# One base address modulo 4096 for all matmul operand tiles of a two-layer decoder trunk

## The chip, the cores and the metric

The kernel runs on one core of one Trainium2 chip. The metric is the device time of one execution in microseconds (us); the time of a kernel is the median of several runs. The profile is of one execution on the same chip.

## What is computed

Two layers over 512 tokens of width 1024, in float32. Each layer is a normed mixer with a residual and a normed feed-forward part with a residual:

```
for l in range(2):
    h = rmsnorm(x, g_pre_mix[l])
    z = h @ w_in[l]                      # 1024 -> 2312: mLSTM q,k,v,o,gates; attention q,k,v
    m_out = mlstm_chunkwise(...)         # 4 heads, 4 chunks of 128 tokens
    a_out = sliding_window_attention(...)# 8 query heads, 2 key heads, window 128, sinks, rotary
    x = x + rmsnorm(concat(m_out, a_out) @ w_out[l], g_post_mix[l])
    h = rmsnorm(x, g_pre_ffn[l])
    u = causal_dwconv(h @ w_up[l], ffn_conv_w[l])       # 1024 -> 5632, width 3
    gate, val = u[:, :2816], u[:, 2816:]
    x = x + rmsnorm((silu(gate) * val) @ w_down[l], g_post_ffn[l])
```

## The kernel before, in words

Every large product is done in split precision. An operand is stored as two tiles, a rounded high part and the rest, and one product takes three matmuls: high by high, high by low, low by high (`mm3`, line 111). So one 128x128 block of weights against 512 columns costs three matmuls of 512 columns each. In the names of an instruction, `acc<-g,w` is a matmul into an accumulator `acc`, with `g` the operand that is streamed through the array (512 columns) and `w` the one that is loaded into it (128 columns).

Weights come by DMA from SP into a `raw` tile; ACT writes the high part and DVE the low part (`wsplit`, lines 98 to 106). The parts land in tiles of four pools, each 128 rows high:

- `hp` (8 tiles `h`) and `wp` (6 tiles `w`), 1024 words per row, and `rp` (3 tiles `raw`), 1024 words;
- `gp` (21 tiles `g`), the main pool, `SLOT` = 1032 words per row (line 29). It holds the transposed activations of the feed-forward part, the outputs of the mixer, part of the gated activations, some weights, and two tiles per layer for the values of the mLSTM (lines 248 and 249), each with two blocks of 4x129 = 516 words. 2x516 = 1032 is why a slot is that wide.

The pools are laid one behind the other in a row of SBUF, so the width of a slot sets the byte address of every tile. In the built program the 21 `g` tiles begin at 40544 + 4128·i, the `h` tiles at 127232 + 4096·i, the `w` tiles at 160000 + 4096·i, and `raw` behind them. So every `h`, `w` and `raw` tile begins at 256 modulo 4096, while the `g` tiles begin at 3680, 3712, 3744, ..., each 32 bytes further modulo 4096 than the one before. A matmul of 512 columns reads both its operands at a multiple of 512 bytes from a tile's start.

The stages of a layer, and which pools their two operands have: the projections by channel (`zchans`, streamed `h`, loaded `w`: `acc<-h,w`) and by token (`ztok`, `acc<-w,h`, 384 columns; `head`, 392 columns); attention and mLSTM in small matmuls between these; the output projection (`outproj`: `acc<-h,g`, `acc<-g,g`, `acc<-w,g`); the up projection (lines 762 to 785: `acc<-g,w`, streamed activations in `g`, 44 blocks of 24 matmuls, the first three blocks in halves of 256 columns); the down projection (lines 801 to 824: streamed weights in `w`, or in `g` for the last five steps of the second half, and the gated activations loaded, `h` for the first four of eleven steps and `g` for the rest; `acc` in the first half, `aux` in the second).

The order on each engine is that of the code; a tile that is wanted waits until the earlier user of its slot is done. POOL issues some small DMAs (`g<-wk`, `g<-g`: halves of the queries and keys moved to other partitions, lines 384 and 400). The descriptors of POOL's DMAs stand in a scratch at the bottom of SBUF, 16 KB in each partition.

Of the kernel before, what the change touches and what calls it, by code (L numbers as in the profile page):

```python
# [8 lines left out]
F32 = mybir.dt.float32  # L9
# [9 lines left out]
NT = 4  # L19
DFF = 2816  # L20
NK2 = 11
NTAIL = 5
# products of the mixer's projections between the steps of the gates, before attention, and between those of the mLSTM
GF = (8, 3, 4, 6)
START = 34
MF = (3, 2, 3, 3, 2)
EPS = 1e-6
NEG = -1e30
SLOT = 1032
WRK = 520  # L30

# columns of the constants
C_ID = 0
C_TRI = 128
C_SEL = 256
# [3 lines left out]
C_MCAU = 528  # L39
C_N = 656  # L40

# columns of the parameters of a layer
P_QK = 0
P_FF = 20
P_SINK = 152
# [5 lines left out]
def tile_hymba_trunk(ctx: ExitStack, tc, x, wch, wta, wtb, wout, wup, wdn, par, gv, mhg, cst, rope, out):  # L51
    nc = tc.nc
    NOSYNC = mybir.DependencyInfo(mybir.DependencyClass.NoSync, mybir.DependencyReason.DATA)

    def after(ins, prev):
        if prev is not None:
            tc.add_manual_dep(ins.ins, prev.ins.name, NOSYNC, reason="slots")
        return ins

    keep = ctx.enter_context(tc.tile_pool(name="keep", bufs=1))  # L60
    gp = ctx.enter_context(tc.tile_pool(name="gp", bufs=21))
    hp = ctx.enter_context(tc.tile_pool(name="hp", bufs=8))
    wp = ctx.enter_context(tc.tile_pool(name="wp", bufs=6))
# [8 lines left out]
    def nm(s):  # L72
        cnt[0] += 1
        return f"{s}_{cnt[0]}"

    def slot(dt=F32, pool=None):
        pool = pool or gp
        if pool is gp:
            t = gp.tile([128, SLOT], dt, tag="g", name=nm("g"))
        elif pool is hp:  # L80
            t = hp.tile([128, 1024], dt, tag="h", name=nm("h"))
        else:
            t = wp.tile([128, 1024], dt, tag="w", name=nm("w"))
        return t

    def work(dt=F32):
        return wk.tile([128, WRK], dt, tag="wk", name=nm("wk"))

# [6 lines left out]
    def small(n, tag):  # L95
        return sp.tile([128, n], F32, tag=tag, name=nm(tag), bufs=1 if n >= 16 else 4)
# [17 lines left out]
    def split_evac(ps, hi, lo):  # L114
        i = nc.scalar.activation(hi, ps, AF.Copy)  # L115
        return i, nc.vector.tensor_tensor(lo, ps, hi.bitcast(F32), ALU.subtract)

    # constants
    cs = keep.tile([128, C_K], F32, name="cs")
    ident = cs[:, C_ID:C_ID + 128]  # L120
    tri = cs[:, C_TRI:C_TRI + 128]
# [29 lines left out]
    def gload(l, i, eng=None, gate=None):  # L151
        g = gbp.tile([128, D], F32, tag="gb", name=nm("gb"))
        after((eng or nc.gpsimd).dma_start(g, gv[l, i:i + 1, :].to_broadcast([128, D])), gate)
        return g
# [57 lines left out]
    def layer_consts(l, gate):  # L212
        pt = keep.tile([128, P_N], F32, tag=f"par{l}", name=f"par{l}")
        after(nc.gpsimd.dma_start(pt, par[l]), gate)
        gh = keep.tile([128, 512], F32, tag="gh", name=f"gh{l}")
        after(nc.gpsimd.dma_start(gh, mhg[l:l + 1, :].to_broadcast([128, 512])), gate)
        ns = keep.tile([128, 8], F32, tag=f"ns{l}", name=f"ns{l}")
        nc.gpsimd.tensor_scalar(ns, pt[:, P_SINK:P_SINK + 8], -1.0, None, ALU.mult)
        return pt, gh, ns
# [13 lines left out]
    def head_weights(l, units, gate, gate2=None):  # L233
        return [wsplit(wta[l, u], 784, wp if u < 2 else gp, gate, gate2)[0] for u in units]
# [4 lines left out]
    def start_layer(l, gate, uA=None):  # L239
        y = Layer()  # L240
        y.l = l
        y.uA = uA or head_weights(l, range(4), gate)
        y.pt, y.gh, y.nsink = layer_consts(l, gate)
        rc = slot()
        after(nc.gpsimd.dma_start(rc[:, :1024], rope), gate)
        y.rcos, y.rsin = rc[:, 0:512], rc[:, 512:1024]
        y.avt = slot()[:, :512].rearrange("p (c d) -> p c d", c=4)
        va = [slot() for _ in range(2)]
        y.vaug = [va[c // 2][:, (c % 2) * 516:(c % 2) * 516 + 516].rearrange("p (h e) -> p h e", h=4) for c in range(NT)]
        for c in range(NT):  # L250
            after(nc.gpsimd.memset(y.vaug[c][:, :, 128:129], 1.0), gate)
        y.hps = {}
        y.gt = small(32, "gt")[:, :].rearrange("p (g h c) -> p g h c", g=2, h=4)
        return y
# [98 lines left out]
            yield  # L353
        return done(ps)

    # the part with the swapped halves is done while the next projection runs
    def rotary(y, ps, outs):
        r0 = work()
        nc.scalar.activation(r0[:, :512], ps, AF.Copy)
        r1 = work()  # L360
        for b in range(4):
            s = (b ^ 1) * 32
            nc.sync.dma_start(r1[b * 32:b * 32 + 32, :512], r0[s:s + 32, :512])
        nc.vector.tensor_tensor(r0[:, :512], ps, y.rcos, ALU.mult)

        def finish():
            nc.gpsimd.tensor_tensor(r1[:, :512], r1[:, :512], y.rsin, ALU.mult)
            outs(r0, r1)
        return finish

    # the queries of a head take 128 rows, the high parts in their own half and the low parts in the other; the keys
    # stand in both halves
    def zchans(y, hT):
        y.qa = [[slot(F32R) for _ in range(2)] for _ in range(2)]
        k2 = slot()
# [50 lines left out]
    def ztok(y, hT, gidx):  # L426
        if gidx == 0:
            y.sg = [slot() for _ in range(2)]
        banks = [acc() for _ in range(NT)]
        for u in range(4):  # L430
            w = wsplit(wtb[y.l, gidx * 4 + u], 768, wp, eng=nc.gpsimd if gidx == 0 and u == 1 else None)[0]
            for c in range(NT):
                for kq in range(2):
                    k = 2 * u + kq
                    mm3(banks[c][:, :384], hTk(hT, k, c * 128, c * 128 + 128),
                        [w[a][:, kq * 384:kq * 384 + 384] for a in range(2)], k == 0, k == 7)
                    yield
        for c in range(NT):
            s = y.sg[c // 2][:, (c % 2) * 512:(c % 2) * 512 + 512]
            if gidx == 0:  # L440
                nc.scalar.activation(
                    y.vaug[c][:, 2:4, 0:128], banks[c][:, 0:256].rearrange("p (h e) -> p h e", h=2), AF.Copy)
                nc.scalar.activation(s[:, 0:128], banks[c][:, 256:384], AF.Tanh, scale=0.5)
            else:
                nc.scalar.activation(s[:, 128:512], banks[c][:, 0:384], AF.Tanh, scale=0.5)
                nc.vector.scalar_tensor_tensor(s, s, 1.0, y.gh, ALU.add, ALU.mult)

    # ---- attention of 4 heads in one block of 128 queries, in steps.  A query sees 128 keys: those of its own
    # block up to itself and those of the block before behind its own place, so both share a square of scores.
    class Att:  # L450
        pass

# [67 lines left out]
            o = (i % 2) * 256  # L520
            split_evac(po[:, o:o + 256], m[:, kv * 256:kv * 256 + 256], m[:, 512 + kv * 256:512 + kv * 256 + 256])

    # ---- mLSTM by chunks, in steps
    def hd(t, h, c):
        p = h % 2
        return t[64 * p:64 * p + 64, (h // 2) * 512 + c * 128:(h // 2) * 512 + c * 128 + 128]
# [99 lines left out]
        y.mix[c][0] = m  # L626
        split_evac(ps, m[:, 0:512], m[:, 512:1024])

    # ---- output projection of one block of tokens, in two steps
    def outproj(y, c, step, ps=None):  # L630
        if step == 0:
            ps = [acc() for _ in range(2)]
        for k in ((4, 5, 6, 7), (0, 1, 2, 3))[step]:
            m = [y.mix[c][k // 4][:, a * 512 + (k % 4) * 128:a * 512 + (k % 4) * 128 + 128] for a in range(2)]
            for hf in range(2):
                mm3(ps[hf], m, [y.wo[k][a][:, hf * 512:hf * 512 + 512] for a in range(2)], k == 4, k == 3)
        return ps

    # ---- FFN
    def conv3(y, ps, j):  # L640
        u = work()
        cw = y.pt[:, P_FF + 3 * j:P_FF + 3 * j + 3]
        nc.scalar.activation(u[:, :512], ps, AF.Copy, scale=cw[:, 2:3])  # L643
        for d in range(1, 3):
            nc.vector.scalar_tensor_tensor(  # L645
                u[:, d:512], ps[:, 0:512 - d], cw[:, 2 - d:3 - d], u[:, d:512], ALU.mult, ALU.add)
        return u
# [17 lines left out]
    hs[2] = prenorm_a(2, gb)  # L665
    hs[3] = prenorm_a(3, gb)
    y = start_layer(0, sq[3], uA)
    head(y, hT, 0, (0, 1))
    head(y, hT, 1, (0, 1))
# [10 lines left out]
    for l in range(L):  # L680
        y.mix = [[None, None] for _ in range(NT)]

        # ---- mixer: attention between the projections
        fill = Filler(zchans(y, hT), ztok(y, hT, 0))
        gates(y, fill)
        its = [(b, kv) for kv in range(2) for b in range(NT)]
# [15 lines left out]
                att4(y, b, kv, aos[kv, b // 2])  # L702
        fill.run()

        # ---- mixer: mLSTM between the last projection, output projection
        fill = Filler(ztok(y, hT, 1))
        Ev, kw, nr = {}, {}, {}
        Ev[0] = ml1(y, 0)
# [43 lines left out]
            if c < NT - 1:  # L752
                prenorm_b(c - 1, hs[c - 1], hT2)

        # ---- FFN, up
        G = [[None] * NK2 for _ in range(2)]
        first = {}

# [16 lines left out]
        for i in range(2 * NK2):  # L775
# [10 lines left out]
            s = work()  # L786
# [6 lines left out]
            o = [G[a][k2][:, (i % 2) * 512:(i % 2) * 512 + 512] for a in range(2)]  # L793
            _, lastg = split_evac(s[:, :512], o[0], o[1])

        # ---- FFN, down
        gpost = gload(l, 3)
        gpre = gload(l + 1, 0) if l + 1 < L else None
        banks = [[acc() for _ in range(NT)], None]
# [7 lines left out]
        for hf in range(2):  # L807
            if hf:
                banks[1] = [psum() for _ in range(NT)]
            for k2 in range(NK2 - (NTAIL if hf else 0)):  # L810
                w, _ = wsplit(wdn[l, hf, k2], 1024, wp)
# [7 lines left out]
        if more:  # L819
            hT = new_hT(hp)  # L820
            y = start_layer(l + 1, gate)
# [85 lines left out]
```

## Time and profile before

| | |
|---|---|
| time, median of 3 runs | 1154.56 us (1154.49 to 1154.7) |
| span of the profiled execution | 1152.6 us |
| PE (TensorE) busy | 1125.3 us, 98% |
| weight loads (PEld) busy | 928.6 us, 81% |
| DVE busy | 667.9 us, 58% |
| ACT busy | 461.1 us, 40% |
| POOL busy | 82.6 us, 7% |
| HBM traffic | 93 GB/s over the span |

The profile gives the span of its execution and no other time of it; the median lies 2.0 us above that span, which is what stands ahead of the first instruction and behind the last. The end of a matmul in the trace is modelled and overlaps the next one's start, so the pace of a stream is read from starts: from the start of one group of the timeline to the start of the next, divided by the number of matmuls in the group.

### The profile page before, as it was taken

The page shows a single profiled execution, that of the slowest core. Times are in us where ns is not written, and L with a number is a line of the kernel's source. Part 1 is how long each engine was busy: PE and PEld are TensorE (multiplying, and loading weights), DVE is VectorE, ACT ScalarE, POOL GpSimd, SP SyncE. Part 2 cuts the span into 40 slices and gives each one's busy share as a digit, 9 for nine tenths or more (in the row PEclk, how much of TensorE's full clock was granted, in tenths as well). Part 3 has the DMA queues.
Part 4 walks back from the last instruction along what each step waited for, and adds up shares of the span by engine and source line. Part 5 has one row for each costly group of instructions (what it writes and reads, how often), then busy time and mean ns, then how long its engine had stood idle before and what let it go on. Part 6 is the DMA issues. An engine that isn't in the chain of part 4 may idle for free.

```text
span 1152.6 us, 14332 instructions
## 1 busy us (share of the span) xinstructions
PE 1125.3 (98%) x5440; PEld 928.6 (81%) x5440; DVE 667.9 (58%) x1086; ACT 461.1 (40%) x890; POOL 82.6 (7%) x142
## 2 busy tenths in 40 slices
PE   6989999999999999999999999999999999999997
PEld 6867888988888888888897787889888888888886
DVE  5589875566565565223557797556565655652223
ACT  5445563444334343223344456444343333431221
POOL 2131011100000000000103210110000000000001
PEclk9989999999999999999999899999999999999999
DMA  7333340232233332234224234202322233222321
GB/s 262 110 96 97 106 143 19 86 110 92 92 100 102 92 92 92 100 101 124 79 92 118 70 106 162 77 19 87 96 92 92 93 97 103 92 92 92 96 87 73
DMA packets 34453, 113.17 MB, mean 98 GB/s; under 512 B 4449, under 2 KB 4609, under 8 KB 34385
## 3 DMA queue, kind: packets, MB, share of 16 engines
q1 hardware_dynamic: 31152, 103.51, 28.3%
q0 software_dynamic: 3088, 8.24, 2.6%
q8 instruction: 43, 0.70, 0.2%
q10 hardware_dynamic: 144, 0.52, 0.1%
q14 instruction: 26, 0.20, 0.1%
HBM read 104.91 MB, written 2.10 MB: 93 GB/s over the span
## 4 chain that ended last, share of the span: by engine, by line
PE 90%; DVE 3%; DMA 2%; ACT 2%; issue 2%; POOL 1%; SPq 0%; DVEq 0%; POOLq 0%; ACTq 0%
PE acc L111 72%; PE aux L111 11%; PE aux L510 1%; PE aux L178 1%; DVE wk L393 1%; PE aux L468 1%; PE aux L566 1%; DMA wk<-wk 1%; PE aux L469 1%; DMA g<-in_cst_dram 1%; PE aux L546 0%; PE aux L496 0%; DMA x<-in_x_dram 0%; ACT wk L481 0%; DMA g<-wk 0%
## 5 line engine op out<-in xcount | busy, mean ns | idle before, releaser
L111 PE MATMUL acc<-g,w 128*128 128x512 f32 (+1 forms) x2256 | 491.1, 379 | 0.0
L111 PEld LDWEIGHTS acc<-g,w 128*128 128x128 f32 x2256 | 403.8, 188 | 86.2
L105 DVE TENSOR_TENSOR w<-raw,w 128x1024 fp32r<-128x1024 f32 (+2 forms) x156 | 186.0, 1194 | 278.8 <-ACT w L103 278.6
L103 ACT ACTIVATE w<-raw 128x1024 fp32r<-128x1024 f32 (+2 forms) x162 | 167.5, 1034 | 338.9 <-PE acc L111 297.2
L111 PE MATMUL acc<-w,h 128*128 128x384 f32 (+2 forms) x672 | 144.4, 362 | 0.4 <-DVE h L185 0.2
L645 DVE SCALAR_TENSOR_TENSOR wk<-acc,par,wk 128x511 f32<-128x511 f32 (+1 forms) x176 | 131.3, 746 | 3.0
L111 PEld LDWEIGHTS acc<-w,h 128*128 128x128 f32 x672 | 118.7, 190 | 14.7 <-issue 4.3
L111 PE MATMUL acc<-h,w 128*128 128x512 f32 x432 | 107.9, 402 | 0.0
L111 PEld LDWEIGHTS acc<-h,w 128*128 128x128 f32 x432 | 80.8, 192 | 17.5 <-issue 1.5
L111 PE MATMUL acc<-w,g 128*128 128x512 f32 x384 | 90.7, 394 | 0.0
L111 PEld LDWEIGHTS acc<-w,g 128*128 128x128 f32 x384 | 72.1, 188 | 16.9
L198 POOL TENSOR_SCALAR rs<-ss 128x1 f32<-128x1 f32 x16 | 5.4, 339 | 762.3 <-ACT junk L193 762.3
L643 ACT ACTIVATE wk<-acc,par 128x512 f32<-128x512 f32 x88 | 59.0, 671 | 0.0
L111 PE MATMUL aux<-g,g 128*128 128x512 f32 x240 | 56.3, 394 | 0.0
L111 PEld LDWEIGHTS aux<-g,g 128*128 128x128 f32 x240 | 45.0, 188 | 10.5
L111 PE MATMUL acc<-h,g 128*128 128x512 f32 x192 | 46.1, 397 | 0.1
L115 ACT ACTIVATE g<-wk 128x512 fp32r<-128x512 f32 x28 | 17.7, 632 | 68.2 <-DVE wk L788 68.2
L111 PE MATMUL aux<-w,h 128*128 128x512 f32 x192 | 43.9, 389 | 0.0
L111 PEld LDWEIGHTS acc<-h,g 128*128 128x128 f32 x192 | 35.6, 188 | 8.5 <-ACT g L115 0.5
L111 PEld LDWEIGHTS aux<-w,h 128*128 128x128 f32 x192 | 36.0, 188 | 7.6
L170 DVE SCALAR_TENSOR_TENSOR wk<-x,rs,gb 128x512 f32<-128x512 f32 x32 | 22.7, 749 | 28.9 <-POOL rs L165 28.9
L111 PE MATMUL acc<-g,g 128*128 128x512 f32 x144 | 35.0, 397 | 0.0
(178 smaller groups left out, 1025.4 us busy)
## 6 DMA issues: line engine op xcount, KB each, us to landing
raw<-in_wup_dram SPq DMA_DIRECT2D x88, 512.0 KB, 3.5
raw<-in_wdn_dram SPq DMA_DIRECT2D x44, 512.0 KB, 3.5
raw<-in_wch_dram SPq DMA_DIRECT2D x18, 512.0 KB, 3.8
raw<-in_wout_dram SPq DMA_DIRECT2D x16, 512.0 KB, 3.5
raw<-in_wtb_dram SPq DMA_DIRECT2D x16, 384.0 KB, 3.2
gb<-in_gv_dram POOLq DMA_DIRECT2D x7, 512.0 KB, 4.3
raw<-in_wta_dram SPq DMA_DIRECT2D x8, 392.0 KB, 4.2
wk<-wk SPq DMA_DIRECT2D x40, 64.0 KB, 2.0
```

The source lines that it names most:

```text
L103: i = nc.scalar.activation(hi[:, :n], raw[:, :n], AF.Copy)
L105: after((eng or nc.vector).tensor_tensor(lo[:, :n], raw[:, :n], hi[:, :n].bitcast(F32), ALU.subtract), gate2)
L111: i = nc.tensor.matmul(o, ls[a], rs[b], start=first and n == 0, stop=last and n == 2)
L115: i = nc.scalar.activation(hi, ps, AF.Copy)
L170: st[c] = nc.vector.scalar_tensor_tensor(h[:, :512], xs[c][:, sl], rs, gb[:, sl], ALU.mult, ALU.mult)
L178: nc.tensor.transpose(ps[:, k * 128:(k + 1) * 128], hs[hf][:, k * 128:(k + 1) * 128], ident)
L393: nc.vector.tensor_tensor(o[:, :512], o[:, :512], r1[:, :512], ALU.add)
L468: nc.tensor.matmul(o, q, y.kh[:, ks], start=True, stop=False)
L469: nc.tensor.matmul(o, q, y.kl[:, ks], start=False, stop=True)
L510: y.lastpv = nc.tensor.matmul(aos[k][64 * p:64 * p + 64, o:o + 256], y.avt[:, t.b - 1 + kh, t.kv * 64:t.kv * 64 + 64], t.PT[:, kh * 512 + ...
L643: nc.scalar.activation(u[:, :512], ps, AF.Copy, scale=cw[:, 2:3])
L645: nc.vector.scalar_tensor_tensor(u[:, d:512], ps[:, 0:512 - d], cw[:, 2 - d:3 - d], u[:, d:512], ALU.mult, ALU.add)
```

## The change

`SLOT` becomes 1024 words. The values of the mLSTM no longer fit in two slots, so they get one tile of 2088 words in a pool of their own (`vp`, one buffer), which stands ahead of `gp`. The room for it comes from the scratch of POOL's DMA descriptors, 8192 bytes instead of 16384. `gp` keeps its 21 slots, two of which the values no longer take. Comments go too, so lines move by up to two.

```
-SLOT = 1032
+SLOT = 1024
 WRK = 520
+VAW = 2088
...
+    vp = ctx.enter_context(tc.tile_pool(name="vp", bufs=1))
     gp = ctx.enter_context(tc.tile_pool(name="gp", bufs=21))
...
-        va = [slot() for _ in range(2)]
-        y.vaug = [va[c // 2][:, (c % 2) * 516:(c % 2) * 516 + 516].rearrange("p (h e) -> p h e", h=4) for c in range(NT)]
+        va = vp.tile([128, VAW], F32, tag="va", name=nm("va"))
+        y.vaug = [va[:, c * 516:c * 516 + 516].rearrange("p (h e) -> p h e", h=4) for c in range(NT)]
...
-    nc = _bacc.Bacc("TRN2", target_bir_lowering=False, num_devices=1)
+    nc = _bacc.Bacc("TRN2", target_bir_lowering=False, num_devices=1, dynamic_dma_scratch_size=8192)
```

In the built program the `va` tile begins at 32352, the `g` tiles at 40704 + 4096·i, the `h` tiles at 126720 + 4096·i and the `w` tiles at 159488 + 4096·i. All of `g`, `h`, `w` and `raw` begin at 3840 modulo 4096, which is 256 modulo 512 as `h` and `w` were before.

On PE, DVE, ACT and SP every instruction keeps its place; only the name `va` stands where the values' `g` stood. On POOL one step moves. Before, ahead of the second layer, POOL sets the ones in the values' tiles (line 251) behind the load of the rotary table:

```order
L198 TENSOR_SCALAR rs_4662<-ss_811_4655 128x1
L199 TENSOR_TENSOR rs_4662<-rs_4662,neghalf 128x1
L245 DMA g_4490<-in_rope_dram 128x1024
L251 MEMSET g_4493 128x4 x2
L251 MEMSET g_4494 128x4 x2
L164 TENSOR_SCALAR rs_4670<-ss_4668 128x1
```

After the change, the same step of the second layer, on POOL again:

```order
L155 DMA gb_3904<-in_gv_dram 128x1024
L216 DMA par_4486<-in_par_dram 128x168
L218 DMA gh_4488<-in_mhg_dram 128x512
L253 MEMSET va_4495 128x4 x4
L220 TENSOR_SCALAR ns_4490<-par_4486 128x8
L200 TENSOR_SCALAR rs_4539<-ss_787_4532 128x1
```

The four memsets have moved up past twelve instructions of POOL, the load of the rotary table among them, to stand right behind the loads of the layer's parameters.

## Rows read from the trace of the kernel before

**Rows 1.** The page: span, and the chain of waits by engine.

```profile
span 1152.6 us, 14332 instructions
...
PE 90%; DVE 3%; DMA 2%; ACT 2%; issue 2%; POOL 1%; SPq 0%; DVEq 0%; POOLq 0%; ACTq 0%
```

**Rows 2.** Groups by shape, PE: operation, names, shapes, count | busy us, mean ns.

```profile
L111 PE MATMUL acc<-g,w 128*128 128x512 f32 x1968 | 456.0, 394 | 0.0
L111 PE MATMUL acc<-h,w 128*128 128x512 f32 x432 | 107.9, 402 | 0.0
L111 PE MATMUL acc<-w,g 128*128 128x512 f32 x384 | 90.7, 394 | 0.0
...
L111 PE MATMUL aux<-g,g 128*128 128x512 f32 x240 | 56.3, 394 | 0.0
L111 PE MATMUL acc<-h,g 128*128 128x512 f32 x192 | 46.1, 397 | 0.1
L111 PE MATMUL aux<-w,h 128*128 128x512 f32 x192 | 43.9, 389 | 0.0
L111 PE MATMUL acc<-w,h 128*128 128x512 f32 x192 | 43.9, 389 | 0.0
...
L111 PE MATMUL acc<-g,g 128*128 128x512 f32 x144 | 35.0, 397 | 0.0
L111 PE MATMUL aux<-w,g 128*128 128x512 f32 x96 | 22.5, 393 | 0.0
```

**Rows 3.** Timeline of PE, up and down, first layer: start us, us, operation, count.

```profile
219.12 238.96 PE L111 MATMUL acc<-g,w 128*128 128x256 f32 x1080
457.92 21.96 PE L111 MATMUL acc<-w,h 128*128 128x512 f32 x96
479.72 39.12 PE L111 MATMUL acc<-w,g 128*128 128x512 f32 x168
518.68 21.96 PE L111 MATMUL aux<-w,h 128*128 128x512 f32 x96
540.48 11.21 PE L111 MATMUL aux<-w,g 128*128 128x512 f32 x48
551.53 20.86 PE L111 MATMUL aux<-g,g 128*128 128x512 f32 x89
```

**Rows 4.** Timeline of PE, up and down, second layer.

```profile
784.71 239.93 PE L111 MATMUL acc<-g,w 128*128 128x256 f32 x1080
1024.48 21.95 PE L111 MATMUL acc<-w,h 128*128 128x512 f32 x96
...
1118.14 27.95 PE L111 MATMUL aux<-g,g 128*128 128x512 f32 x120
```

**Rows 5.** Timeline of PE, output projection, and the halves of 256 columns.

```profile
163.27 4.33 PE L111 MATMUL acc<-g,g 128*128 128x512 f32 x18
167.44 1.55 PE L111 MATMUL acc<-w,g 128*128 128x512 f32 x6
...
215.17 3.07 PE L111 MATMUL acc<-g,w 128*128 128x256 f32 x24
218.08 1.28 PE L178 MATMUL aux<-cs,wk 128*128 128x128 f32 x8
```

**Rows 6.** Timeline of PE, projections by channel, second layer.

```profile
600.11 5.66 PE L111 MATMUL acc<-h,w 128*128 128x512 f32 x24
605.61 0.29 PE L287 MATMUL aux<-lf,cs 128*128 128x16 f32 x2
```

**Rows 7.** Timeline of POOL: a pair of its DMAs, and the ones of the values.

```profile
60.72 1.08 POOL L400 DMA_DIRECT2D g<-wk  x2 [2.48 <-DVE wk L399]
...
576.14 0.20 POOL L251 MEMSET g<- 128x4 f32 x4 [0.31 <-PE aux L111]
```

**Rows 8.** The page, DMA issues: count, KB each, median us to landing.

```profile
g<-wk POOLq DMA_DIRECT2D x16, 128.0 KB, 2.6
```

**Rows 9.** Windows: stretch, busy us of PE, PEld, DVE, ACT, POOL, clock, DMA.

```profile
600.00:660.00 60.00, 55.44 (x255) 45.22 (x254) 42.91 (x91) 27.34 (x60) 16.56 (x17) 0.94 0.37 104
```

## The prediction, made before the changed kernel was run

> **What bounds the kernel.** I read the chain of waits first. PE makes up 90% of it [rows 1], so the time is mostly the number of matmuls times the pace at which they start. Then I read the matmuls by the pools of their operands [rows 2] and the timeline of PE stage by stage [rows 3 to 6]. The reader is to see that in the up and down projections one group begins before the modelled end of the one before, so no other engine's work stands between them, and that the pace of these streams still differs. The down projection is the cleanest place. There the same weights are streamed from `w` tiles; only the loaded operand changes, from `h` tiles to `g` tiles. From 457.92 to 479.72 us 96 matmuls with `w,h` start: 21.80 / 96 = 227.1 ns each. From 479.72 to 518.68, 168 with `w,g`: 38.96 / 168 = 231.9 ns. Then `h` again, 518.68 to 540.48: 21.80 / 96 = 227.1 ns, and `g` again, 540.48 to 551.53: 11.05 / 48 = 230.2 ns [rows 3]. The pace goes down, up and down again within one stage, with the pool of the loaded tile. The mean duration in the groups says the same: 389 ns for both `w,h` groups, 393 to 397 ns for the six groups with a `g` [rows 2].
>
> What sets `g` apart is the address. Both operands of a `w,h` matmul begin at 256 modulo 512, whereas a `g` tile begins 32 bytes further per slot. My step is that a matmul whose two operands (and the load that runs beside it) have one address modulo 512 starts about 4.5 ns earlier than one whose operands don't, and that this holds whichever pool the tile is in. After the change that holds for all of them. (One `g` tile in 21 has that address before, too, by its place in the row; I take nothing off for it.)
>
> **The sum.** The matmuls of 512 columns with a `g` operand number 1968 + 384 + 240 + 192 + 144 + 96 = 3024 [rows 2]. The 432 + 192 + 192 = 816 of `h` and `w` alone keep their pace. By stage, over both layers, with 227.1 ns as the pace after:
>
> - Up projection, 1968 matmuls. The stretch of the first layer takes 457.92 − 219.12 = 238.80 us for 1080 matmuls. Of these 96 are halves of 256 columns: 24 + 72 by the loop over the first three blocks, at (218.08 − 215.17) / 24 = 121 ns [rows 5], so 11.6 us. The other 984 take 227.2 us, 230.9 ns each [rows 3]. In the second layer it is (239.77 − 11.6) / 984 = 231.9 ns [rows 4]. Mean 231.4, so 1968 × 4.3 = 8.5 us.
> - Down projection, `acc<-w,g`: of the 384 in the group 48 are the output projection's, so 336 × (231.9 − 227.1) = 1.6 us.
> - Down projection, `aux<-w,g`: 96 × (230.2 − 227.1) = 0.3 us.
> - Down projection, `aux<-g,g`: the last stretch shows 27.95 us for 120 [rows 4]; without the 0.39 us of the last one's own duration that is 27.56 / 119 = 231.6 ns. 240 × 4.5 = 1.1 us.
> - Output projection, 192 + 144 + 48 = 384: (167.44 − 163.27) / 18 = 231.7 ns [rows 5]. 384 × 4.6 = 1.8 us.
>
> Together 13.3 us. All of it is on the path, since in these stages PE is not waiting. The span 1152.6 would become 1139.3; the 2.0 us that the median lies above the span stay, so I predict **1141.3 us**, −1.15%.
>
> What could be late instead once PE is faster: one block of the up projection needs 24 × 227 ns = 5.45 us instead of 5.55, and in this time one weight tile must be loaded and split. This is 2% more demand in a stage whose loads already keep pace with no wait visible. I cost it at nothing; without this cover it would take back at most the 8.5 us of that stage.
>
> **The other edits, each with its cost.** The own tile for the values renames operands on ACT and PE and moves four memsets on POOL up past twelve instructions; they take 0.20 us [rows 7] and nothing needs them for tens of microseconds. Two slots of `gp` become free, so some tiles of `g` may be filled sooner; in a stage where PE is already busy throughout this buys nothing. The values are fp32 operands of small matmuls which go on starting at an address off the others; no change. The first three blocks' 256-column matmuls and the small ones of attention with `g` operands could gain or lose: the trace has no aligned 256-column matmul to read. Bounds: 288 halves and some 500 small ones at ±4.6 ns are ±3.6 us. I take nothing, since at 121 ns for 256 columns the pace is not that of the long streams. The smaller scratch I cost at nothing too: POOL issues at most a few DMAs together, and what it would cost otherwise is a rival below.
>
> The size of the step has a lower bound too. In the projections by channel, where DVE, ACT and POOL work beside `acc<-h,w`, 24 aligned matmuls take 605.61 − 600.11 = 5.50 us, 229.2 ns each [rows 6]. If the up projection, which also streams activations against `w`, came only to that pace, the sum would be 3024 × (231.5 − 229.2) = 7.0 us, for 1147.6 us. I take 227.1, since the output, up and down projections have fewer engines beside PE.
>
> **The skill, weighed.** The rows say that the pace hangs on where the loaded tile lies: 227.1 against 231.9 ns beside the same stream [rows 3]. The Trainium skill, "SBUF — State Buffer", section "Who interferes with whom", says that PE has two read ports of its own, one for the moving operand and one for the weight load, and that "PE and ACT never wait on anyone"; its page "TensorE: Matmul & The Clock Gate", Part 2, says that loading the next tile's weights takes nothing from the running matmul. Taken strictly, addresses would not matter and the time would stay at 1154.6 us. This case's trace disagrees by those 4.8 ns.
>
> **The rivals.**
>
> - *The address is not the cause; no change.* What separates `h` from `g` may be something else that goes with the pool, such as the order in which slots are reused or what is written beside the stream. For it: I compare pools, not addresses. Against it: the pace changes back at once at each of the three borders in the down projection, under the same streamed weights, and every one of the six `g` groups is slow whatever its partner is. Then the 13.3 us don't come: 1154.6 us.
> - *Half the gain.* The common address helps only to the pace of the busier stage: 1147.6 us, as above.
> - *POOL's DMAs begin to wait.* With half the scratch, the second DMA of a pair could be held until the first has landed. Both of a pair are issued within 1.08 us now [rows 7] and one takes 2.6 us to land [rows 8], so such a wait costs about 2.6 − 0.5 = 2.1 us; there are eight pairs of `g<-wk` and two of `g<-g`, and the start of attention, where PE is idle for some 4.6 us of 60 in the second layer [rows 9], hangs on them. All ten on the path are 21 us: 1141.3 + 21 = 1162 us, slower than before. It decides from about seven pairs on (7 × 2.1 = 14.7 > 13.3). Against it: a DMA of 128 KB is small beside the loads of 512 KB that the same queue issues back to back. The Trainium skill, "SBUF — State Buffer", section "SBUF size: 192, 224, or 256?", gives 16 KiB per partition as the carve-out for the rings of such descriptors, which is a reason to ask; no run here shows a ring that is full.
> - *The clock.* In 600 to 660 us the granted clock is 0.94 on average [rows 9], so some of the stretch ran at 1.2 instead of 2.4 GHz, at the time when PE waits for attention to begin. Sixty times 0.06 × 2 = 7 us ran at the half clock, which cost at most half of that, 3.6 us. Where such a stretch falls can shift with the start of the stage: ±3.6 us, in the range and not in the sum.
>
> **How the numbers follow.** Chances: the forecast near 1141.3 us 0.75, half the gain 0.13, no change 0.07, POOL's waits 0.03, and 0.02 for something that I don't see, half of it slower. The likeliest case alone, with the bounds of the small matmuls or the clock, is 1137 to 1145. To hold 8 in 10 the range must reach well into "half the gain"; I give 1136 to 1148. A measurement of this kernel can tell about 0.2% (2.3 us) from no change. Faster by more than that: 0.75 + 0.13 + 0.01, and a little of the rival without change, whose edits could still bring something: 0.90. Within 0.2%: 0.06. Slower: 0.04.
>
> **What would show it.** If the step is right, the timeline of the down projection loses its borders: `acc<-w,g` and `aux<-w,g` start every 227 ns like `w,h`; the up projection's 1080 matmuls take about 235 us in each layer; the groups with a `g` have a mean near 389 ns. The groups of `h` and `w` alone stay at 389 ns. POOL's pairs of DMAs still take 1.08 us to issue. It is wrong if the up projection keeps 231 ns; if it falls only to 229, the second rival holds; if POOL's rows at lines 386 and 402 grow by 2 us each, the third.

## The result and the profile after

The changed kernel takes 1140.94 us (median of 4 runs, 1138.7 to 1141.38) against 1154.63 us before: the ratio is 0.9875, 95% interval 0.9863 to 0.9887. The prediction was 1141.3 us, 1136 to 1148.

The page of the kernel after, span and PE, against [rows 1]. PE is busy for 15.6 us less than the 1125.3 us of before, and the loads of its weights as long as before.

```profile
span 1136.8 us, 14332 instructions
...
PE 1109.7 (98%) x5440; PEld 928.5 (82%) x5440; DVE 667.4 (59%) x1086; ACT 461.0 (41%) x890; POOL 83.3 (7%) x142
```

The groups by shape of the kernel after answer to [rows 2]; lines are two higher.

```profile
L113 PE MATMUL acc<-g,w 128*128 128x512 f32 x1968 | 446.5, 390 | 0.0
L113 PE MATMUL acc<-h,w 128*128 128x512 f32 x432 | 107.4, 401 | 0.0
L113 PE MATMUL acc<-w,g 128*128 128x512 f32 x384 | 88.7, 390 | 0.0
...
L113 PE MATMUL aux<-g,g 128*128 128x512 f32 x240 | 55.0, 390 | 0.0
L113 PE MATMUL acc<-h,g 128*128 128x512 f32 x192 | 45.2, 393 | 0.1
L113 PE MATMUL acc<-w,h 128*128 128x512 f32 x192 | 43.8, 389 | 0.0
L113 PE MATMUL aux<-w,h 128*128 128x512 f32 x192 | 43.8, 390 | 0.0
L113 PE MATMUL acc<-g,w 128*128 128x256 f32 x288 | 35.8, 285 | 0.0
L113 PE MATMUL acc<-g,g 128*128 128x512 f32 x144 | 34.6, 393 | 0.0
L113 PE MATMUL aux<-w,g 128*128 128x512 f32 x96 | 22.1, 390 | 0.0
```

The six groups of 512 columns with a `g` lose 9.5, 2.0, 1.3, 0.9, 0.4 and 0.4 us, 14.5 us together; the two `w,h` groups stay within 0.1 us and `acc<-h,w` within 0.5.

The timeline of PE in the down projection of the first layer, after (start us, us, operation, count), against [rows 3]:

```profile
451.89 21.92 PE L113 MATMUL acc<-w,h 128*128 128x512 f32 x96
473.65 38.24 PE L113 MATMUL acc<-w,g 128*128 128x512 f32 x168
511.73 21.92 PE L113 MATMUL aux<-w,h 128*128 128x512 f32 x96
533.49 11.04 PE L113 MATMUL aux<-w,g 128*128 128x512 f32 x48
544.37 20.57 PE L113 MATMUL aux<-g,g 128*128 128x512 f32 x90
```

The borders are gone. From start to start the four stretches take 21.76 / 96 = 226.7, 38.08 / 168 = 226.7, 21.76 / 96 = 226.7 and 10.88 / 48 = 226.7 ns.

This profiled execution is the quickest of the four runs after (1138.7 us; the others took 1140.86 to 1141.38). Its span falls by 15.8 us, while the medians differ by 13.7. A part of what it has more is the clock: in the stretch from 30 to 100 us, in which PE waits for attention to begin, 0.98 was granted on average and not 0.95. Before, then after (stretch, busy us of PE, PEld, DVE, ACT, POOL, granted clock, DMA):

```profile
30.00:100.00 70.00, 63.88 (x304) 52.19 (x303) 51.94 (x108) 29.90 (x65) 18.61 (x19) 0.95 0.35 93
```

```profile
30.00:100.00 70.00, 64.57 (x311) 52.44 (x309) 52.83 (x110) 31.12 (x73) 19.43 (x20) 0.98 0.34 93
```

The timeline of PE in this stretch, before and then after, shows that the clock is the smaller part (start us, us, operation, count, idle before and its releaser):

```profile
70.29 0.44 PE L468 MATMUL aux<-g,g 128*128 128x128 f32 x1 [4.85 <-DMA g<-wk]
...
78.90 2.34 PE L111 MATMUL acc<-h,w 128*128 128x512 f32 x9
```

```profile
69.35 0.30 PE L470 MATMUL aux<-g,g 128*128 128x128 f32 x1 [4.14 <-DMA g<-wk]
...
77.70 2.33 PE L113 MATMUL acc<-h,w 128*128 128x512 f32 x9
```

When attention begins, the run after is already 0.94 us ahead, after a shorter wait for a DMA (4.14 and not 4.85 us) and a slightly earlier start. By the second row it is 1.20 us ahead, so the matmuls between, where the clock differs, account for some 0.3 us.

### The profile page after: what moved, and what is told of

The parts are those of the page before. It is cut to its first block, busy times and chain, and to the rows that moved or that the text cites. A ratio compares the mean times of both kernels' runs of the same rounds, so it can differ in the third digit from the quotient of the medians.

```text
span 1136.8 us, 14332 instructions
## 1 busy us (share of the span) xinstructions
PE 1109.7 (98%) x5440; PEld 928.5 (82%) x5440; DVE 667.4 (59%) x1086; ACT 461.0 (41%) x890; POOL 83.3 (7%) x142
## 4 chain that ended last, share of the span: by engine, by line
PE 88%; DVE 2%; issue 1%; ACT 1%; DMA 1%; SPq 0%; POOL 0%; DVEq 0%; POOLq 0%; ACTq 0%
PE acc L113 71%; PE aux L113 11%; PE aux L512 1%; PE aux L180 1%; PE aux L470 1%; PE aux L568 1%; PE aux L471 1%; DVE wk L395 1%; PE aux L548 0%; PE aux L498 0%; ACT wk L483 0%; DMA g<-wk 0%; PE aux L560 0%; DVE wk L492 0%; PE aux L604 0%
## 5 line engine op out<-in xcount | busy, mean ns | idle before, releaser
L113 PE MATMUL acc<-g,w 128*128 128x512 f32 (+1 forms) x2256 | 482.0, 376 | 0.0
L113 PEld LDWEIGHTS acc<-w,h 128*128 128x128 f32 x672 | 118.4, 189 | 14.5 <-issue 4.3
L113 PE MATMUL acc<-g,g 128*128 128x512 f32 x144 | 34.6, 393 | 0.0
```

Source lines behind the costliest of these rows:

```text
L113: i = nc.tensor.matmul(o, ls[a], rs[b], start=first and n == 0, stop=last and n == 2)
```

## The experiments

The theory is that the pace of a long stream hangs on the address of the operand that is streamed against that of the operand that is loaded. The rivals: the two slots that became free, or the scratch; the address of an operand by itself; and, once the theory stood, other forms of it. A kernel that ran only once is read by its groups, where busy us over the count is the pace, and its time is given beside them.

**The addresses alone, with the other two edits undone.** The values' tile takes its room from two slots of the main pool, not from the scratch.

```
-    gp = ctx.enter_context(tc.tile_pool(name="gp", bufs=21))
+    gp = ctx.enter_context(tc.tile_pool(name="gp", bufs=19))
-  dynamic_dma_scratch_size=8192
+  dynamic_dma_scratch_size=16384
```

> The changed kernel with 19 main slots instead of 21 and a descriptor scratch of 16 KB as before. So the slots that other tiles can use, and the scratch, are as before the change; only the addresses (all operand tiles at one address modulo 4096) and the values' own tile are new. Theory (the common address is the cause): about 1141 us, 0.987 of before, the streams with a g operand at 227 ns. Rival (the two slots that became free, or the scratch, brought the gain): about 1154 us, g streams at 231 to 232 ns.

1148.15 us (1146.73 to 1148.6), ratio 0.9939, interval 0.9924 to 0.9954: between the two. The streams do what the theory says:

```profile
L113 PE MATMUL acc<-g,w 128*128 128x512 f32 x1968 | 446.5, 389 | 0.0
...
L113 PE MATMUL acc<-w,g 128*128 128x512 f32 x384 | 88.7, 389 | 0.0
```

Most of what is lost lies at the border of the layers. In the window from 560 to 600 us PE is busy for 35.88 of 40 us, and the projections by channel of the second layer begin at 599.62 us; after the change PE is busy throughout that window and they begin at 592.23. That is 7.39 us later; 0.96 us of it is there before the border (545.33 against 544.37 us at the start of `aux<-g,g`), so the border costs 6.4 us. The timeline of PE in this experiment:

```profile
545.33 26.50 PE L113 MATMUL aux<-g,g 128*128 128x512 f32 x115
...
599.62 5.66 PE L113 MATMUL acc<-h,w 128*128 128x512 f32 x24
```

The timeline of ACT in this experiment, then after the change, shows the start of it (start us, us, operation, count, idle before and its releaser):

```profile
563.66 1.61 ACT L105 ACTIVATE g<-raw 128x784 fp32r<-128x784 f32 x2 [13.14 <-PE aux L113]
```

```profile
546.34 0.86 ACT L105 ACTIVATE g<-raw 128x784 fp32r<-128x784 f32 x1 [2.15 <-DMA raw<-in_wta_dram]
```

ACT waits 13.14 us for PE to let go of slots, with a weight of the next layer's first projection, and the norms at the end of the layer are queued behind it. So my expectation was wrong in its premise: 19 slots are not what the kernel before had. There the values' two slots serve other tiles while no values are alive, which is so in the feed-forward part, and all 21 are wanted at the border. The run shows that the address alone brings the pace, whatever the scratch is; it doesn't measure the two free slots.

**The stagger put back, the other edits kept.** This one does.

```
-SLOT = 1024
+SLOT = 1032
-VAW = 2088
+VAW = 2064
-  dynamic_dma_scratch_size=8192
+  dynamic_dma_scratch_size=8064
```

> The changed kernel with slots of 1032 words again, each 32 bytes further modulo 4096 than the last; the own tile for the values and the two free slots are kept, the scratch is 8064 bytes. Theory (common address): back to about 1154 us, g streams at 231 to 232 ns on average, h,w streams still at 227. Rival (free slots or scratch): about 1141 us.

1156.47 us (10 runs, 1155.16 to 1158.71), ratio 1.0015, interval 1.0005 to 1.0025. The streams are as before, `h,w` ones among them:

```profile
L113 PE MATMUL acc<-g,w 128*128 128x512 f32 x1968 | 458.1, 395 | 0.0
...
L113 PE MATMUL aux<-w,h 128*128 128x512 f32 x192 | 43.9, 389 | 0.0
```

So the free slots and the smaller scratch bring nothing; the whole gain goes with the stagger. The 0.15% above before are in the streams too (458.1 against 456.0 us): each slot lies as far from the `w` tiles as before the change (119456 bytes for the first), but with the values gone from the pool other tiles stand in the slots, so the streams meet other disagreements.

**One offset for all: 128 bytes, then 512.** A tile between the main pool and those behind it moves all `h`, `w` and `raw` tiles against all `g` tiles.

```
     gp = ctx.enter_context(tc.tile_pool(name="gp", bufs=21))
+    pd = ctx.enter_context(tc.tile_pool(name="pd", bufs=1))
+    pd.tile([128, 32], F32, tag="pd", name="pd")      # 32 words; 128 words for 512 bytes
     hp = ctx.enter_context(tc.tile_pool(name="hp", bufs=8))
```

> The changed kernel with 128 bytes put between the main pool and the pools behind it: every g tile has one address modulo 4096 and every h, w and raw tile another, 128 bytes on. Theory, in the form that the address of the one operand against the other counts: streams with one g operand and one h or w operand slow to 231 to 234 ns (in the trace of before, the stretches of the up projection where the streamed tile stood 128 bytes below the w tiles started every 233 ns), while g,g and h,w streams stay at 227 ns; some 1153 us or more. Rival (what counts is that an operand stands at 256 modulo 512 itself): h,w streams slow too, g,g streams stay.

> The same with 512 bytes between. Theory (address modulo 512): no stream changes, 227 ns everywhere, 1139 to 1141 us. Rival (the address must agree modulo 4096): streams with a g and an h or w operand slow to 231 ns or more, some 1152 us.

1156.42 us with 128 bytes, 1141.37 us with 512. The groups with 128:

```profile
L115 PE MATMUL acc<-g,w 128*128 128x512 f32 x1968 | 458.6, 395 | 0.0
...
L115 PE MATMUL acc<-w,g 128*128 128x512 f32 x384 | 90.8, 394 | 0.0
...
L115 PE MATMUL aux<-g,g 128*128 128x512 f32 x240 | 55.1, 390 | 0.0
...
L115 PE MATMUL aux<-w,h 128*128 128x512 f32 x192 | 43.9, 389 | 0.0
```

`acc<-g,w` is slow again, at 458.6 / 1968 = 233.0 ns, while `g,g` and `w,h`, whose two operands moved together, keep 55.1 and 43.9 us. This is the clearest of the runs: within one execution only the streams that mix the pools are slow. With 512 bytes `acc<-g,w` is back at 446.5 us, so agreement modulo 4096 isn't needed.

**All operand tiles moved together by 32 bytes.** The same tile, of 8 words, ahead of the main pool.

> The changed kernel with 32 bytes put ahead of the main pool, so that all operand tiles move together: one address modulo 4096 still, but 288 modulo 512 and not 256. Theory (the address of one operand against the other counts): nothing changes, every stream at 227 ns, 1139 to 1142 us. Rival (an operand's own address counts, 256 modulo 512 being a good one): all long streams slow down, h,w among them, to 231 ns or more, over 1155 us.

1140.91 us, and the groups of after:

```profile
L115 PE MATMUL acc<-g,w 128*128 128x512 f32 x1968 | 446.5, 389 | 0.0
```

An operand's own address, moved here by 32 bytes, has no part in it; the rival fell.

**Other offsets: 480, 224, 256, then 64 and 192 bytes.** The same edit with 120, 56, 64, 16 and 48 words.

> 480 bytes between the main pool and the pools behind it, so that a g tile stands 32 bytes above an h or w tile modulo 512. Theory (a function of the relative address modulo 512, to be read off the trace of before): there the stretches of the up projection with the streamed tile 32 bytes above started every 236 ns; so acc<-g,w at 235 to 236 ns, acc<-w,g at 232 or more, g,g and h,w at 227; 1158 to 1160 us. Rival (any disagreement costs the same 4.5 to 6 ns): 231 to 233 ns, about 1154 us.

> 224 bytes between, so that a g tile stands 288 bytes above an h or w tile modulo 512. Theory (a function of the relative address modulo 512): the stretches of before with this offset in the up projection started every 226.8 ns, so this offset costs nothing there although the addresses disagree: acc<-g,w at 227 ns, and what remains is what the down projection makes of the opposite sign; 1140 to 1146 us. Rival (any disagreement costs): 231 to 233 ns, about 1154 us.

> 256 bytes between. Theory (relative address modulo 512): the two times that before had this offset (some ten starts in the down projection) it ran at 227 to 228 ns, so half of 512 may agree as well as 512 does: 227 to 229 ns, 1140 to 1147 us. Rival (only agreement modulo 512 is fast): 231 ns or more, 1152 us or more.

> 64 bytes between the main pool and the pools behind it. After the offsets 128, 224 and 480 (all 232.9 to 233.3 ns) and 256 and 512 (226.7 ns): if only agreement modulo 256 is fast, acc<-g,w starts every 233 ns and the time is 1155 to 1158 us. Rival (there is a shorter period, 64 bytes, that 224 and 480 missed and 128 contradicts only in part, or the cost grows with the offset): 227 to 231 ns, under 1152 us.

> 192 bytes between, the mirror image of 64. With 64 the streams that stream g and load w started every 233.3 ns and those that stream w and load g every 229.2 ns. Theory (the pace is a function of streamed address less loaded address, modulo 256): the two change places: acc<-g,w at 229 ns (busy near 452 us), acc<-w,g at 233 ns (busy near 91 us), and as the up projection is much the larger the time is about 1147 us. Rival (the pool decides, or the size of the stage, and the sign has no part in it): acc<-g,w at 233 ns again, 1155 to 1157 us.

The times were 1157.79, 1157.39, 1139.6, 1155.53 and 1149.98 us. The two groups that matter, from the groups by shape, with 480 and then 224 bytes:

```profile
L115 PE MATMUL acc<-g,w 128*128 128x512 f32 x1968 | 459.5, 395 | 0.0
...
L115 PE MATMUL acc<-w,g 128*128 128x512 f32 x384 | 91.2, 396 | 0.0
```

```profile
L115 PE MATMUL acc<-g,w 128*128 128x512 f32 x1968 | 459.5, 395 | 0.0
...
L115 PE MATMUL acc<-w,g 128*128 128x512 f32 x384 | 91.2, 396 | 0.0
```

With 256, with 64 and with 192:

```profile
L115 PE MATMUL acc<-g,w 128*128 128x512 f32 x1968 | 446.5, 389 | 0.0
...
L115 PE MATMUL acc<-w,g 128*128 128x512 f32 x384 | 88.7, 389 | 0.0
```

```profile
L115 PE MATMUL acc<-g,w 128*128 128x512 f32 x1968 | 459.5, 395 | 0.0
...
L115 PE MATMUL acc<-w,g 128*128 128x512 f32 x384 | 89.7, 392 | 0.0
```

```profile
L115 PE MATMUL acc<-g,w 128*128 128x512 f32 x1968 | 450.8, 391 | 0.0
...
L115 PE MATMUL acc<-w,g 128*128 128x512 f32 x384 | 91.2, 395 | 0.0
```

Put together, with streamed address less loaded address modulo 256 worked out from the offset, and the pace as busy us over the count:

| offset | `acc<-g,w`: streamed less loaded, pace | `acc<-w,g`: streamed less loaded, pace |
|---|---|---|
| 0, 256, 512 | 0, 226.9 ns | 0, 231.0 ns |
| 64 | 192, 233.5 | 64, 233.6 |
| 128 | 128, 233.0 | 128, 236.5 |
| 192 | 64, 229.1 | 192, 237.5 |
| 224, 480 | 32, 233.5 | 224, 237.5 |

(In the second column each figure holds some 4 ns of the ends of short stretches. From start to start within a stretch `acc<-w,g` takes 226.7, 229.3, 232.4, 233.4 and 233.3 ns, from the first row to the last.) Three things follow. 256 bytes do as well as 512, so the period is 256 as far as multiples of 32 were tried, and 480 and 224, which are the same modulo 256, agree to the tenth. Every offset tried that isn't a multiple of 256 costs something. And the sign counts: 64 and 192 change places when the streamed and the loaded operand do, as the last expectation said, though the time came to 1149.98 and not 1147 us, since the streams `acc<-w,g` and `acc<-h,g` paid (2.5 and 1.1 us more than after the change). Two expectations were wrong. I had read paces for single offsets off the trace of before, 236 ns for 32 and 226.8 for 288 bytes, and both ran at 233.5: the stretches of before mix two tiles with two offsets, so they don't show what one offset costs.

**The high and the low part of the weights 128 bytes apart.**

```
-            t = wp.tile([128, 1024], dt, tag="w", name=nm("w"))
+            t = wp.tile([128, 1056], dt, tag="w", name=nm("w"))
-VAW = 2088
+VAW = 2064
-  dynamic_dma_scratch_size=8192
+  dynamic_dma_scratch_size=7936
```

> The changed kernel with w slots of 1056 words, so that neighbouring w tiles lie 128 bytes apart modulo 256: of the high and low part of one weight tile one agrees with g and h and the other doesn't (the room comes from the scratch, 7936 bytes, and the values' tile). Theory (what counts is the operand that is streamed against the operand that is loaded beside it, one matmul at a time): only the matmuls that load or stream the part that disagrees are late, so about half of them: streams with a w operand at 229 to 231 ns, acc<-g,w busy near 453 us; g,g and h,g streams stay at 227; about 1147 to 1150 us. Rival (one disagreeing tile in a stream slows the whole stream): w streams at 233 ns, above 1156 us, h,w among them.

1156.92 us:

```profile
L113 PE MATMUL acc<-g,w 128*128 128x512 f32 x1968 | 457.0, 395 | 0.0
...
L113 PE MATMUL acc<-h,g 128*128 128x512 f32 x192 | 45.3, 393 | 0.1
L113 PE MATMUL aux<-w,h 128*128 128x512 f32 x192 | 44.8, 394 | 0.0
```

457.0 / 1968 = 232.2 ns: nearly the price of a stream in which everything disagrees, and not the half that I had expected. `acc<-h,g` has no `w` and stays at 45.3 us, `aux<-w,h` has one and slows for the first time. The starts in this trace, put beside the addresses of the built program, show where the rest comes from. Of the 1968 matmuls `acc<-g,w`, 460 agree both with the tile loaded for them and with the one loaded beside them for the next matmul; the next one starts 226.9 ns later on average. Where only the tile loaded beside disagrees (628) it takes 233.3 ns, where only their own does (629) 233.7, and where both do (251) 234.2. So one disagreeing tile makes two matmuls late: the one that runs while it is loaded, and the one it serves. Which read it is that waits, the streamed one or the load, and why, these runs don't show; the loads' own mean is 188 ns before and after the change and 189 here.

## Why the prediction was right

- *The step.* It held as forecast: matmuls that differ in the operands' relative address differ in pace, and they lose that difference when the addresses agree. The load that runs beside a matmul counts too, as the forecast had it in brackets (233.3 against 226.9 ns). The forecast said modulo 512; the runs show 256.
- *The sum.* 13.3 us forecast, 14.5 us measured in the groups. The up projection was forecast at 8.5 and gave 9.5 us (456.0 to 446.5). The difference is the pace after, 226.7 ns where I took 227.1: 0.4 ns over 3024 matmuls is 1.2 us. The medians moved by 13.7 us, 0.8 less than the groups. The halves of 256 columns, which I took at nothing, take back 0.4 us, see below; the rest is less than the spread of the runs after the change. So that the forecast of 1141.3 us came within 0.4 us of the median is in part luck: a sum 1.2 us too small met a rest that I had not counted.
- *Nothing else becomes late.* It held. PE has no idle time in the up projection with 2% more demand on loads and splits, and the groups with `h` and `w` alone didn't move.
- *The free slots and the scratch at nothing.* The run with the stagger put back shows just that (1.0015). What I had not seen is the other side: two slots fewer cost 6.4 us at the border of the layers.
- *Half the gain* (1147.6 us): the up projection runs at 226.7 ns, while the projections by channel keep the 229.2 ns of [rows 6] after the change, (597.73 − 592.23) / 24. I had put that down to more engines at work beside PE; no run tests it, and why aligned matmuls are slower there stays open. The timeline of PE after the change:

```profile
592.23 5.66 PE L113 MATMUL acc<-h,w 128*128 128x512 f32 x24
597.73 0.29 PE L289 MATMUL aux<-lf,cs 128*128 128x16 f32 x2
```

- *No change*: the rival that something else goes with the pool fell with the offsets. They show that PE's streams depend on where the two operands lie, 226.9 against 233.5 ns, with the same pools and the same order. The Trainium skill ("SBUF — State Buffer", "Who interferes with whom") gives PE independent read ports for the moving operand and the weight load; taken as strictly as the prediction weighed it, the two paces would be one. Here the measurement decides.
- *POOL's waits*: they didn't come. Its pair of DMAs after the change, against [rows 7]:

```profile
59.77 1.08 POOL L402 DMA_DIRECT2D g<-wk  x2 [2.48 <-DVE wk L401]
```

- *The clock*: one stretch at the low level was shorter in the profiled execution, which is the quickest of the four, for some 0.3 us; it was rightly kept out of the sum.

## What to carry to other kernels

Where PE is busy throughout, compare the pace of its long streams by the pools of their operands, from start to start; a difference of some per cent under the same work is worth a look at the tiles' byte addresses. Give every pool that holds matmul operands a tile width that is a multiple of the period (here 256 bytes), and put odd-sized tiles in a pool of their own ahead of or behind them all: 32 words between two such pools cost the whole gain here. Before a pool gives up slots for that, look at who waits for its slots at the borders of stages.

## What the runs showed that I had not expected

- The 128x256 matmuls of the up projection's first blocks go the other way: 35.8 us for 288 when addresses agree (mean 285 ns), 35.4 us before the change, and 34.6 us with an offset of 64 bytes. So agreement is not the best for every shape. Before, then with 64 bytes:

```profile
L111 PE MATMUL acc<-g,w 128*128 128x256 f32 x288 | 35.4, 282 | 0.0
```

```profile
L115 PE MATMUL acc<-g,w 128*128 128x256 f32 x288 | 34.6, 280 | 0.0
```

- The price of an offset is not graded by its size: 32 bytes cost as much as 128 (233.5 and 233.0 ns), and 64 cost 2.2 or 6.6 ns by its sign.
- Only multiples of 32 bytes were tried, and all operands were 4 bytes wide. Whether the period is the same for narrower ones stays open.
